# Layer 0 of a hybrid diffusion backbone: all tokens transposed first, more landing tiles, shift and scale wholly on TensorE

## The chip, the core and the metric

The kernel runs on one core of one Trainium2 chip. The engines are TensorE (PE; PEld is its weight load), VectorE (DVE), ScalarE (ACT), GpSimd (POOL) and SyncE (SP), which here issues the DMAs. The metric is the device time of one execution in microseconds, lower is better; times below are of the kernel before.

## What is computed

Four layers over 256 latent tokens and 256 context tokens of width 2048 in fp32. Layer i normalises (RMSNorm), applies shift and scale that come from a conditioning vector, mixes tokens (0: Fourier, 1: mLSTM, 2: attention, 3: Fourier), projects and adds with a gate. The start, which is all that the change touches, is this part:

```python
sc = jax.nn.silu(c)                                    # and sc_ctx = silu(c_ctx)
shift, scale, gate = jnp.split(sc @ ada_w[i] + ada_b[i], 3, axis=-1)
hx = _rmsnorm(x, norm_g[i]) * (1.0 + scale[:, None]) + shift[:, None]
...
def _fnet_branch(h, w_gate, w_out):
    return (_fourier_mix(h) * jax.nn.silu(h @ w_gate)) @ w_out
```

`ada_w[0]` is 2048 x 6144; its shift and scale columns are 33.5 MB, and no product with `w_gate` can start on a row of h before that row's shift and scale are known.

## The kernel before

Every large product is done by `gemm`: fp32 values are split into a high and a low part of a faster format (h and l of the activations, wh and wl of the weights), and three matmuls (h with wh, h with wl, l with wh) are added up. The reduction over 2048 runs in 16 tiles `kt`, taken as 8 pairs `k2`; one pair needs one weight tile of 512 KB, which `make_w` loads, splits on ScalarE (wh) and VectorE (wl), and hands out. A group of 512 output columns has four accumulator banks, so a pair is 24 matmuls of one group, called products here.

Layer 0 starts so: the conditioning vector is spread to all partitions (`spread`), the tokens `xt` are loaded in four tiles, their squares are summed on ScalarE (L585), and the reciprocal root r0 scales all of them on VectorE (L639). Then a loop over the 8 pairs (L640) makes shift and scale for the pair, in two pieces (SC and SH). A piece on TensorE, `ada_pe`, loads four landing tiles `araw` of 512 KB, multiplies them with the padded vector `cpad` (L187, 16 matmuls, each recorded as two by the profile), copies the result (`ar`), transposes it (L195) and adds up on VectorE. A piece on VectorE, `ada_dve`, loads four tiles of a transposed copy of the weights (`ada_t`) and makes two passes over each (L217). Both use the same four `araw` tiles. For pairs 2, 4 and 6 (`DV0`) the shift is made on VectorE, so 13 pieces are TensorE's and 3 are VectorE's.

What follows for a pair is the generator `turned(k2)`: for each of its two `kt` four transposes of the tokens (L615), the modulation from PSUM on ScalarE (`u`, L618), the split (L360, L361), and then the products of the pair before it. It is queued in the weave `fill`, which is advanced by one step for every 1/0.8 of a yield of the next pair's pieces. A second weave, `mixes`, advances the Fourier mixes of column blocks 0 to 2 (`mixed(j)`, eight yields each: four banks with L498, then two parities with L531, the first with L536) at 0.9 steps a yield. After pair 7 the rest of group 0 (`first`, with its last two pairs together, four times 12 products) and group 1 run, with what is left of the mixes woven in, and from there the gate's columns (`ga0`) on VectorE. `done_g` (L602) ends each column block of a group.

TensorE's program order is written by hand, as these generators yield; on the other engines a scheduler orders instructions. SP issues all DMAs in one order, and waits where a tile is still in use. Lines below are those of the kernel before; in the changed kernel the same statements stand some 10 to 40 lines lower (L187 is L197, L195 is L205, L298 is L308, L498 is L509, L531 is L542, the token transposes L615 are L637).

Of the kernel before, what the change touches and what calls it, by code (L numbers as in the profile page):

```python
# [14 lines left out]
P = 128  # L15
# [7 lines left out]
ARAW, WRAW, WHL = 4, 4, 3  # L23

DV0 = (2, 4, 6)

NPE1, CORE1, ATT = 4, 0.4, 1.2
MIX3, MIX0, MIX1, FR0, BR0, AR0 = 0.55, 0.9, 0.7, 0.8, 0.34, 0.17
# [23 lines left out]
def _build(tc, nc, top, A, out):  # L52
# [119 lines left out]

    def ada_pe(l, s, c, cpad, place):


        ps = bank()
        for k2 in range(2):
            raws = []
            for kq in (2 * k2, 2 * k2 + 1):
                pp, tag, bufs = next(place[0])  # L180
                raw = pp.tile([P, 2, 512], F32, tag=tag, name="araw", bufs=bufs)
                Q.dma_start(raw, A["ada_p"][l, s * 8 + c, kq])
                raws.append(raw.rearrange("p a b -> p (a b)").rearrange("p (q n) -> p q n", q=4))
            for i, rv in enumerate(raws):
                kq = 2 * k2 + i
                for q in range(4):
                    T.matmul(ps[32 * q:32 * q + 32, :256], cpad[:, 4 * kq + q, :], rv[:, q, :],  # L187
                             start=kq == 0, stop=kq == 3)
            yield 1
        r = ap_.tile([P, 256], F32, tag="ar", name="ar", bufs=1)  # L190
        S.copy(r, ps[:, :256])
        yield 1
        pt = bank()
        for i in range(2):
            T.transpose(pt[:, 128 * i:128 * i + 128], r[:, 128 * i:128 * i + 128], ident)  # L195
# [69 lines left out]
    def gemm(hl, orient, t0, t1, done, first=False, used=None, halves=False, begin=None):  # L265
# [46 lines left out]
        for k2 in range(2 if begin else 0, 6):  # L312
# [16 lines left out]
        wa, wb = next_w(), next_w()  # L329
        for kt in range(12, 16):  # L330
            hl[kt]
        yield "made"
        make_w()
        if halves:
            for s in range(2):
                for b in range(nb):
                    for kt in range(12, 16):
                        one(b, kt, wa if kt < 14 else wb, s)
# [5 lines left out]
        for b in range(nb):  # L344
            for kt in range(12, 16):
                one(b, kt, wa if kt < 14 else wb)
                if kt == 13:
                    yield
            done(b, banks[b][:, :n])
            yield  # L350
# [214 lines left out]
    with ExitStack() as st:  # L565
# [13 lines left out]
        for j in range(4):  # L579
# [3 lines left out]
            for i in range(4):  # L583
                junk = p0.tile([P, 512], F32, tag="mu2", name="junk", bufs=2)
                S.activation(junk, x[:, i, :], AF.Square, accum_out=ss[:, i, j:j + 1])  # L585
# [18 lines left out]

        with ExitStack() as st2:
            pf = pool(st2, "l0f", reuse_waits="tile")
            first = gemm(hl, "A", 0, 512, done_g, first=True)

            def turned(k2):

                for kt in (2 * k2, 2 * k2 + 1):
                    j, i = divmod(kt, 4)
                    ps = bank()
                    for t in range(4):
                        T.transpose(ps[:, 128 * t:128 * t + 128], xt[j][:, t, 128 * i:128 * i + 128], ident)  # L615
                    u = p0.tile([P, 512], F32, tag="mu2", name="u", bufs=2)
                    for s in range(2):
                        S.activation(u[:, 256 * s:256 * s + 256], ps[:, 256 * s:256 * s + 256], AF.Identity,  # L618
                                     scale=ada[:, 0, SC, s, kt:kt + 1], bias=ada[:, 0, SH, s, kt:kt + 1])
                    hl[kt] = split_into(kt, u)  # L620
                    yield
                if 0 < k2 <= 6:
                    for _ in range(4):
                        next(first)
                        yield
# [9 lines left out]
            mixes = Weave()  # L635
            slots = repeat((ap_, "araw", ARAW))
            for j in range(4):  # L637
                for i in range(4):
                    V.tensor_scalar(xt[j][:, i, :], xt[j][:, i, :], r0[:, i:i + 1], None, ALU.mult)  # L639
            for k2 in range(8):  # L640
                for s in (SC, SH):
                    for _ in ada_dve(0, s, 2 * k2, 2, 2) if s == SH and k2 in DV0 else ada_pe(0, s, k2, cpad, [slots]):
                        fill.give(FR0)
                        mixes.give(MIX0)
                fill.finish(f"t{k2 - 1}")
                fill.add(f"t{k2}", turned(k2))
                if k2 == 0:
                    Q.dma_start(cst[:, C_CD:], A["cst"][:, C_CD:])
# [6 lines left out]
            run(first, MIX1)  # L655
            order = [(s, j) for s in (SC, SH) for j in range(4)]
# [10 lines left out]
        place[0] = repeat((pa, "praw", 2))  # L667
# [703 lines left out]
```

## Time and profile before

| | |
|---|---|
| median of 3 runs | 2152.68 us (2150.70 to 2155.58) |
| the profiled execution | 2155.34 us, span 2153.5 us, mean granted clock 0.987 |
| first product of layer 0 (L298) | 54.61 us after the span's start |
| last piece of shift and scale on PE | 152.00 to 153.00 us |
| last `done_g` of group 0, of group 1 | 173.65 and 221.94 us |
| PE's waits for landing tiles, to 222 us | 12.7 us in 14 waits |

The span is the profiled time between the first and the last instruction; the rest of the execution's time lies around it. The rows of the page and of the trace on which the argument rests stand in the prediction.

### The profile page before, as it was taken

What the parts mean: (1) busy time and instruction counts of PE and PEld (TensorE: products, weight loads), DVE (VectorE), ACT (ScalarE), POOL (GpSimd) and SP (SyncE); (2) the same over time, 40 slices, a digit from 0 to 9 for tenths busy, and PEclk for the clock granted to TensorE, in tenths of its full rate; (3) what the DMA queues carried; (4) which work ended last, traced back from release to release, by engine and by line L of the source; (5) the groups of instructions that cost most, each with busy time, mean ns of one, the idle gap of its engine ahead of it and who ended that gap; (6) DMA issues with size and microseconds to landing.
All of it is one profiled execution on the core that took longest, in us unless ns stands there. A gap on an engine that the chain in (4) does not pass through costs nothing. (4 is left out here: it accounts for less than half of the span.)

```text
span 2153.5 us, 29391 instructions
## 1 busy us (share of the span) xinstructions
PE 2091.3 (97%) x11190; PEld 1725.9 (80%) x11190; DVE 1527.3 (71%) x2793; ACT 812.2 (38%) x1338; POOL 19.3 (1%) x29
## 2 busy tenths in 40 slices
PE   6899999999999999999999999999999999999998
PEld 2668777788788888888888888888787777999986
DVE  4867888856787787799666678765645665567666
ACT  4332242223333324232332343223336544545444
POOL 0000000000000000000000000000000000000000
PEclk7999999999999999999999999999999999999999
DMA  9775778872465565477668667983243454564464
GB/s 349 275 265 191 250 276 282 322 271 95 153 209 166 199 224 179 162 250 254 202 207 305 226 235 280 335 312 107 88 137 124 141 176 138 173 195 138 153 194 147
DMA packets 126127, 451.52 MB, mean 210 GB/s; under 512 B 14224, under 2 KB 16784, under 8 KB 123296
## 3 DMA queue, kind: packets, MB, share of 16 engines
q1 hardware_dynamic: 125696, 448.71, 61.0%
q8 instruction: 88, 1.44, 0.3%
q10 hardware_dynamic: 288, 0.92, 0.1%
q14 instruction: 55, 0.45, 0.1%
HBM read 435.91 MB, written 13.66 MB: 209 GB/s over the span
## 5 line engine op out<-in xcount | busy, mean ns | idle before, releaser
L257 DVE TENSOR_TENSOR wl<-wraw,wh 128x1024 fp32r<-128x1024 f32 x400 | 489.1, 1224 | 404.6 <-ACT wh L256 393.4
L298 PE MATMUL acc<-h,wh 128*128 128x512 f32 (+1 forms) x1936 | 689.3, 356 | 6.1 <-ACT h L395 3.9
L256 ACT CAST wh<-wraw 128x1024 fp32r<-128x1024 f32 x400 | 419.1, 1049 | 724.4 <-PE acc L298 581.4
L298 PE MATMUL acc<-l,wh 128*128 128x512 f32 (+1 forms) x1936 | 671.7, 347 | 3.0 <-DVE l L396 1.8
L298 PE MATMUL acc<-h,wl 128*128 128x512 f32 (+1 forms) x1936 | 670.4, 346 | 1.3 <-DVE wl L257 1.1
L298 PE MATMUL acc<-wh,h 128*128 128x512 f32 x1024 | 427.0, 417 | 3.5 <-DVE xn L1019 2.2
L298 PEld LDWEIGHTS acc<-h,wh 128*128 128x128 f32 x1936 | 367.8, 190 | 61.9 <-issue 11.2
L298 PEld LDWEIGHTS acc<-l,wh 128*128 128x128 f32 x1936 | 367.3, 190 | 51.2 <-DVE l L396 3.5
L298 PEld LDWEIGHTS acc<-h,wl 128*128 128x128 f32 x1936 | 367.9, 190 | 45.7 <-DVE wl L257 2.3
L298 PE MATMUL acc<-wh,l 128*128 128x512 f32 x1024 | 401.2, 392 | 0.5 <-DVE l L396 0.5
L298 PE MATMUL acc<-wl,h 128*128 128x512 f32 x1024 | 399.7, 390 | 0.0
L217 DVE SCALAR_TENSOR_TENSOR araw<-araw,cb 128x1024 f32<-128x1024 f32 x300 | 364.7, 1223 | 12.0 <-DMA araw<-in_ada_t_dram 9.8
L298 PEld LDWEIGHTS acc<-wh,h 128*128 128x128 f32 x1024 | 192.8, 188 | 52.0 <-issue 14.5
L298 PEld LDWEIGHTS acc<-wl,h 128*128 128x128 f32 x1024 | 193.0, 188 | 44.6 <-issue 8.4
L298 PEld LDWEIGHTS acc<-wh,l 128*128 128x128 f32 x1024 | 192.5, 188 | 42.8 <-DVE l L396 1.3
L217 DVE SCALAR_TENSOR_TENSOR ajunk<-araw,cb 128x1024 f32<-128x1024 f32 x172 | 209.8, 1220 | 0.0
L187 PE MATMUL xb<-araw,cpad 128*32 128x256 f32 x672 | 56.7, 439 | 15.4 <-DMA araw<-in_ada_p_dram 12.7
L187 PEld LDWEIGHTS xb<-araw,cpad 128*32 128x32 f32 x672 | 17.6, 116 | 44.9 <-DMA araw<-in_ada_p_dram 26.9
L395 ACT ACTIVATE h<-mu,ada 128x256 fp32r<-128x256 f32 x80 | 36.9, 502 | 35.9 <-DVE mu L394 35.9
L848 PE MATMUL xb<-v,wt 128*128 128x256 f32 x192 | 46.7, 379 | 0.0
L453 ACT ACTIVATE sq<-rn 128x256 f32<-128x256 f32 (+1 forms) x48 | 24.7, 515 | 56.1 <-DVE rn L447 54.3
L908 ACT ACTIVATE jk<-yp 128x256 f32<-128x256 f32 x32 | 13.3, 417 | 78.8 <-DVE yp L906 78.8
(223 smaller groups left out, 1480.3 us busy)
## 6 DMA issues: line engine op xcount, KB each, us to landing
araw<-in_ada_t_dram SPq DMA_DIRECT2D x300, 512.0 KB, 5.2
wraw<-in_w1in_dram SPq DMA_DIRECT2D x128, 512.0 KB, 4.4
araw<-in_ada_p_dram SPq DMA_DIRECT2D x84, 512.0 KB, 5.4
wraw<-in_w2in_dram SPq DMA_DIRECT2D x80, 512.0 KB, 3.5
wraw<-in_w0g_dram SPq DMA_DIRECT2D x32, 512.0 KB, 5.5
wraw<-in_w0o_dram SPq DMA_DIRECT2D x32, 512.0 KB, 5.7
wraw<-in_w1o_dram SPq DMA_DIRECT2D x32, 512.0 KB, 7.0
wraw<-in_w2o_dram SPq DMA_DIRECT2D x32, 512.0 KB, 4.2
```

Source lines behind the costliest of these rows:

```text
L187: T.matmul(ps[32 * q:32 * q + 32, :256], cpad[:, 4 * kq + q, :], rv[:, q, :], start=kq == 0, stop=kq == 3)
L217: V.scalar_tensor_tensor(o, rv, 1.0, cb[:, v + 2 - nv, part], ALU.mult, ALU.mult, accum_out=am[:, v, i, hf:hf + 1])
L256: S.copy(wh, raw)
L257: pace.append(V.tensor_tensor(wl, raw, wh.bitcast(F32), ALU.subtract).ins)
L298: T.matmul(o, lhsT, rhs, start=start, stop=stop)
L395: S.activation(h[:, c], u, AF.Identity, bias=ada[:, l, SH, s, kt:kt + 1])
L453: S.activation(sq[:, c], rn[:, b, c], AF.Square)
L848: T.matmul(po[:, :256], wt[:, 128 * k:128 * k + 128], c.v[:, k, 256 * hh:256 * hh + 256], start=k == 0, stop=k == nb - 1)
L908: S.activation(jk, ys, AF.Square, accum_out=c.ssq[:, 4 * hh + i:4 * hh + i + 1])
```

## The change

It concerns layer 0 up to the end of group 1.

- All shift and scale pieces of layer 0 are made by `ada_pe`; `DV0` is gone.
- `begin(0, ...)` weaves `turn(j)` into the two pieces of pair 0: it scales the tokens (half on ScalarE), transposes all 16 tiles and parks them as `xT` in the buffers of the later h tiles. `modulated(k2)` reads them from there.
- In `begin(k2)` the two pieces of pair k2 are woven with the products of pair k2-1 (six at a step, four steps), and otherwise with steps of the mixes. The weight tile is made at its beginning. `modulated(k2)` comes last.
- Landing tiles: pairs 0 to 2 cycle through six extra tiles (`l0l`) and the four `araw`; pairs 3 to 7 through the four `araw` and those buffers of l tiles 10 to 15 that are still free, each of which takes its 512 KB as two DMAs (`land_l`).
- The mixes of blocks 0, 1 and 2 are queued after pairs 3, 4 and 5 rather than 1, 3 and 5, at 1.0 step a yield, and what is left of them runs with group 0's last pair and group 1.
- Group 0 keeps one pair (`tail=1`) rather than two for its end.
- Half of the sums of squares go to VectorE, and the table for the root is loaded before the last token tile.

```diff
-DV0 = (2, 4, 6)
+ARAW, WRAW, WHL, LAND = 4, 4, 3, 6
-MIX3, MIX0, MIX1, FR0, BR0, AR0 = 0.55, 0.9, 0.7, 0.8, 0.34, 0.17
+MIX3, MIX0, MIX1, BR0, AR0 = 0.55, 1.0, 0.7, 0.34, 0.17
...
+    def land_l(kt):
+        def get(src):
+            raws = [hlp.tile([P, 512], F32, tag=f"l{k}", name=f"lraw{k}") for k in (kt, kt + 1)]
+            for i in range(2):
+                Q.dma_start(raws[i], src[:, i, :])
+            return raws
+        return get
...
-                junk = p0.tile([P, 512], F32, tag="mu2", name="junk", bufs=2)
-                S.activation(junk, x[:, i, :], AF.Square, accum_out=ss[:, i, j:j + 1])
+                if i % 2:
+                    junk = p0.tile([P, 512], F32, tag="mu2", name="junk", bufs=2)
+                    S.activation(junk, x[:, i, :], AF.Square, accum_out=ss[:, i, j:j + 1])
+                else:
+                    junk = ap_.tile([P, 1024], F32, tag="junk", name="ajunk", bufs=1)[:, :512]
+                    V.scalar_tensor_tensor(junk, x[:, i, :], 1.0, x[:, i, :], ALU.mult, ALU.mult,
+                                           accum_out=ss[:, i, j:j + 1])
+            if j == 2:
+                S.activation(dummy, ss[:, 1, 2:3], AF.Sqrt)
...
+        first = gemm(hl, "A", 0, 512, done_g, first=True, tail=1)
+        def turn(j):
+            for t in range(4):
+                if t % 2:
+                    S.activation(xt[j][:, t, :], xt[j][:, t, :], AF.Copy, scale=r0[:, t:t + 1])
+                else:
+                    V.tensor_scalar(xt[j][:, t, :], xt[j][:, t, :], r0[:, t:t + 1], None, ALU.mult)
+            for i in range(4):
+                ps = bank()
+                for t in range(4):
+                    T.transpose(ps[:, 128 * t:128 * t + 128], xt[j][:, t, 128 * i:128 * i + 128], ident)
+                x = hlp.tile([P, 512], F32, tag=f"h{4 * j + i}", name=f"xT{4 * j + i}")
+                (S.copy if i % 2 else V.tensor_copy)(x, ps)
+                xT.append(x)
+        def modulated(k2):
+            for kt in (2 * k2, 2 * k2 + 1):
+                u = p0.tile([P, 512], F32, tag="mu2", name="u", bufs=2)
+                for s in range(2):
+                    c = slice(256 * s, 256 * s + 256)
+                    S.activation(u[:, c], xT[kt][:, c], AF.Identity, scale=ada[:, 0, SC, s, kt:kt + 1],
+                                 bias=ada[:, 0, SH, s, kt:kt + 1])
+                hl[kt] = split_into(kt, u)
+        def begin(k2, places):
+            make_w()
+            place = [places]
+            for n, _ in enumerate(chain(*(ada_pe(0, s, k2, cpad, place) for s in (SC, SH)))):
+                if k2 == 0:
+                    if n % 2:
+                        turn(n // 2)
+                elif n in (1, 2, 5, 6):
+                    next(first)
+                else:
+                    mixes.give(MIX0)
+            modulated(k2)
+        with ExitStack() as st2:
+            pl = pool(st2, "l0l", reuse_waits="tile")
+            places = cycle([land(pl, "land", LAND)] * LAND + [araws] * ARAW)
+            for k2 in range(3):
+                begin(k2, places)
...
-            for k2 in range(8):
-                for s in (SC, SH):
-                    for _ in ada_dve(0, s, 2 * k2, 2, 2) if s == SH and k2 in DV0 else ada_pe(0, s, k2, cpad, [slots]):
-                        fill.give(FR0)
-                        mixes.give(MIX0)
-                fill.finish(f"t{k2 - 1}")
-                fill.add(f"t{k2}", turned(k2))
-                if k2 in (1, 3, 5):
-                    mixes.add("m", mixed(k2 // 2))
-            fill.finish("t7")
+            for k2 in range(3, 8):
+                spare = [land_l(kt) for kt in (10, 12, 14) if kt > 2 * k2]
+                begin(k2, cycle([araws] * ARAW + spare))
+                if k2 in (3, 4, 5):
+                    mixes.add("m", mixed(k2 - 3))
             while mixes.q:
                 fill.add("mix", mixes.q.pop(0)[1])
             fill.add("mix", mixed(3))
+            fill.step()
             run(first, MIX1)
```

First place: TensorE from pair 1's scale piece to the first products. Before, the pair's second piece is followed by token transposes of pair 1 (L615), banks of the first mix (L498) and then the products of `kt` 0:

```order
L187 MATMUL xb<-araw,cpad 32x256 x16
L615 MATMUL xb<-cst,xt 128x128 x4
L498 MATMUL xb<-cst,eo 128x128 x4
L615 MATMUL xb<-cst,xt 128x128 x4
L498 MATMUL xb<-cst,eo 128x128 x4
L195 MATMUL xb<-cst,ar 128x128 x2
L298 MATMUL acc<-h_338,wh 128x512
```

After the change, from the second piece of pair 0 on:

```order
L197 MATMUL xb<-araw,cpad 32x256 x16
L637 MATMUL xb<-cst,xt 128x128 x16
L205 MATMUL xb<-cst,ar 128x128 x2
L637 MATMUL xb<-cst,xt 128x128 x16
L197 MATMUL xb<-araw,cpad 32x256 x16
L308 MATMUL acc<-h_426,wh 128x512
L308 MATMUL acc<-h_426,wl 128x512
L308 MATMUL acc<-l_427,wh 128x512
```

The first products now stand behind three pieces instead of five, and all 64 token transposes stand before them; no mix has begun.

Second place: SP's queue from the last token tiles on. Before (the pieces of pairs 0, 1 and the first of 2, then the first VectorE piece):

```order
L581 DMA xt<-in_xtok_dram 128x2048 x3
L182 DMA araw<-in_ada_p_dram 128x1024 x8
L648 DMA cst<-in_cst_dram 128x1032
L182 DMA araw<-in_ada_p_dram 128x1024 x12
L253 DMA wraw<-in_w0g_dram 128x1024
L210 DMA araw<-in_ada_t_dram 128x1024 x4
L253 DMA wraw<-in_w0g_dram 128x1024 x3
```

After (`araw` stands for the extra landing tiles too, which bear the same name; `lraw` are the halves in l's buffers):

```order
L592 DMA xt<-in_xtok_dram 128x2048 x3
L263 DMA wraw<-in_w0g_dram 128x1024
L175 DMA araw<-in_ada_p_dram 128x1024 x8
L675 DMA cst<-in_cst_dram 128x1032
L263 DMA wraw<-in_w0g_dram 128x1024
L175 DMA araw<-in_ada_p_dram 128x1024 x8
L263 DMA wraw<-in_w0g_dram 128x1024
L175 DMA araw<-in_ada_p_dram 128x1024 x8
L263 DMA wraw<-in_w0g_dram 128x1024
L175 DMA araw<-in_ada_p_dram 128x1024 x4
L184 DMA lraw_721<-in_ada_p_dram 128x512
```

The weight tiles moved ahead of each pair's eight landing tiles, and no `ada_t` tile is left in this stage.

Third place: TensorE behind the last piece. Before, from the last product of pair 5:

```order
L298 MATMUL acc<-l_1094,wh 128x512
L615 MATMUL xb<-cst,xt 128x128 x8
L298 MATMUL acc<-h_1284,wh 128x512
L298 MATMUL acc<-h_1284,wl 128x512
L298 MATMUL acc<-l_1285,wh 128x512
L298 MATMUL acc<-h_1298,wh 128x512
```

After, from the last product of pair 6 (h_1414 is pair 7's first tile):

```order
L308 MATMUL acc<-l_1264,wh 128x512
L205 MATMUL xb<-cst,ar 128x128 x2
L542 MATMUL xb<-fU,cst 128x258 x2
L542 MATMUL xb<-fU,cst 128x126 x2
L542 MATMUL xb<-fU,cst 128x128 x2
L509 MATMUL xb<-cst,eo 128x128 x4
L308 MATMUL acc<-h_1414,wh 128x512
```

Before, pair 6's products and a mix bank stood between pair 7's transposes and its products; now one parity and one bank of mixes do.

More of the change, by code (lines that the diff above doesn't have):

```diff
@@ L177, in ada_pe @@
         for k2 in range(2):
[L178 to L183, printed above, removed]
+            raws = [next(place[0])(A["ada_p"][l, s * 8 + c, kq]) for kq in (2 * k2, 2 * k2 + 1)]
             for i, rv in enumerate(raws):
@@ L336, in gemm @@
                 for b in range(nb):
-                    for kt in range(12, 16):
-                        one(b, kt, wa if kt < 14 else wb, s)
+                    for kt in last:
+                        one(b, kt, ws[kt // 2 - 8], s)
                     if b % 2:
@@ L344, in gemm @@
         for b in range(nb):
-            for kt in range(12, 16):
-                one(b, kt, wa if kt < 14 else wb)
+            for kt in last:
+                one(b, kt, ws[kt // 2 - 8])
                 if kt == 13:
@@ L605, in _build @@
         with ExitStack() as st2:
             pf = pool(st2, "l0f", reuse_waits="tile")
[L607 to L625, printed above, removed]
```

35 lines of the change are left out of this document (19 added, 16 removed).

## The prediction

> **What bounds the kernel now.** I read the page first: busy shares, then the 40 slices.
>
> ```profile
> span 2153.5 us, 29391 instructions
> PE 2091.3 (97%) x11190; PEld 1725.9 (80%) x11190; DVE 1527.3 (71%) x2793; ACT 812.2 (38%) x1338; POOL 19.3 (1%) x29
> ...
> PE   6899999999999999999999999999999999999998
> ...
> PEclk7999999999999999999999999999999999999999
> ...
> GB/s 349 275 265 191 250 276 282 322 271 95 153 209 166 199 224 179 162 250 254 202 207 305 226 235 280 335 312 107 88 137 124 141 176 138 173 195 138 153 194 147
> ```
>
> The reader should see that PE is the bound everywhere but at the start, and that the first slice (54 us) has at once the lowest PE share, the lowest granted clock and the highest transfer rate, 349 GB/s. So I cut the start into stages; the columns are busy time of PE, PEld, DVE, ACT and POOL, then granted clock, DMA share and GB/s.
>
> ```profile
> 10.00:20.00 10.00, 5.61 (x40) 2.19 (x40) 5.22 (x15) 9.13 (x26) 0.00 (x0) 0.80 1.01 410
> 10.00:50.00 40.00, 27.16 (x199) 9.49 (x200) 16.62 (x46) 14.43 (x38) 0.00 (x0) 0.66 0.97 359
> 50.00:100.00 50.00, 43.58 (x309) 32.61 (x308) 39.29 (x93) 20.87 (x43) 0.00 (x0) 0.96 0.79 284
> 100.00:150.00 50.00, 41.23 (x300) 28.43 (x296) 34.50 (x98) 16.70 (x41) 0.00 (x0) 0.90 0.77 269
> 150.00:222.00 72.00, 70.82 (x358) 57.23 (x347) 51.99 (x105) 22.98 (x38) 0.00 (x0) 1.00 0.59 200
> 222.00:2153.50 1931.50, 1904.78 (x10028) 1594.72 (x10026) 1378.42 (x2443) 732.97 (x1170) 19.08 (x25) 1.00 0.60 203
> ```
>
> Between 10 and 150 us PE idles 12.8, 6.4 and 8.8 us, and until 50 us it runs at 0.66 of its clock. From 222 us on it idles 26.7 of 1931.5 us, 1.4%, at full clock. The change touches only work that ends by 222 us; what follows is PE-bound and woven by counts of yields, not by time, so whatever is won or lost at 222 us should arrive at the end unchanged. The transfers are the other resource: 97% busy until 50 us, then only 79% and 77%, though the next 33.5 MB of weights are known from the start. Who holds them back is in the waits of the DMA queue, and what PE waits for in its own (total us, times, longest):
>
> ```profile
> SPq L182 <- PE xb L187: 37.2, 29, 4.4
> SPq L182 <- DVE araw L217: 30.2, 9, 8.0
> ```
>
> ```profile
> PE xb L187 <- DMA araw<-in_ada_p_dram: 12.7, 14, 3.6
> PE xb L531 <- DVE fU L511: 2.5, 3, 1.1
> PE xb L531 <- ACT u L618: 1.8, 1, 1.8
> PE xb L531 <- ACT F L559: 1.8, 1, 1.8
> ```
>
> The queue waits for a landing tile to come free, 37 us for PE's pieces and 30 us for the VectorE pieces, while PE waits 12.7 us for landings. Four landing tiles are the throttle.
>
> **Prices, from the timeline.** (Start, duration, engine, line.)
>
> ```profile
> 54.61 0.51 PE L298 MATMUL acc<-h,wh 128*128 128x512 f32 x1 [2.26 <-ACT wh L256]
> ...
> 71.59 2.03 PE L531 MATMUL xb<-fU,cst 128*128 128x258 f32 x12 [1.84 <-ACT F L559]
> 73.54 1.07 PE L187 MATMUL xb<-araw,cpad 128*32 128x256 f32 x16
> ...
> 80.51 0.50 PE L298 MATMUL acc<-h,wh 128*128 128x512 f32 x1
> ...
> 83.39 0.38 PE L195 MATMUL xb<-cst,ar 128*128 128x128 f32 x2
> 83.70 1.07 PE L187 MATMUL xb<-araw,cpad 128*32 128x256 f32 x16
> 84.70 0.66 PE L615 MATMUL xb<-cst,xt 128*128 128x128 f32 x4
> ...
> 127.47 1.06 PE L498 MATMUL xb<-cst,eo 128*128 128x128 f32 x8
> 128.28 0.47 PE L298 MATMUL acc<-h,wh 128*128 128x512 f32 x1
> ```
>
> Matmuls overlap, so I price by starts. Half a piece of `ada_pe` (two landing tiles) takes 83.70 to 84.70, 1.0 us, and the two transposes 83.39 to 83.70, 0.3: **a piece costs PE 2.3 us**. From 80.51 to 83.39 run 12 products: 0.24 each, 5.8 us for a pair's 24. One Fourier bank takes 0.81, one parity of L531 71.59 to 73.54, 1.95: a mix is 4 x 0.81 + 2 x 1.95 + 0.3 for L536, 7.4 us.
>
> **Part 1, three pieces go from VectorE to TensorE.** PE gains 3 x 2.3 = 6.9 us. VectorE loses 3 x 8 passes over a tile, by this row 1.2 us each; they are hidden now except as holders of landing tiles (the 30.2 us above).
>
> ```profile
> L217 DVE SCALAR_TENSOR_TENSOR araw<-araw,cb 128x1024 f32<-128x1024 f32 x300 | 364.7, 1223 | 12.0 <-DMA araw<-in_ada_t_dram 9.8
> ```
>
> **Part 2, all tokens transposed in pair 0, landing in 10 tiles.** Pair 0 must scale 16 quarter tiles, half on each of two engines, copy 16 banks out, half each, and make the first h and l:
>
> ```profile
> L618 ACT ACTIVATE u<-xb,ada 128x256 f32<-128x256 f32 x32 | 16.4, 564 | 11.1 <-DVE ada L169 8.0 <-PE xb L615 3.0
> ...
> L361 DVE TENSOR_TENSOR l<-u,h 128x512 fp32r<-128x512 f32 x16 | 11.0, 690 | 18.9 <-ACT h L360 18.8
> ...
> L360 ACT CAST h<-u 128x512 fp32r<-128x512 f32 x16 | 9.9, 621 | 0.2
> L585 ACT ACTIVATE junk<-xt 128x512 f32<-128x512 f32 x16 | 9.9, 618 | 4.5 <-DMA xt<-in_xtok_dram 4.5
> ...
> L576 DVE COPY cb<-xb 128x512 f32<-128x512 f32 x8 | 5.1, 683 | 0.6 <-PE xb L236 0.6
> ```
>
> ```profile
> 19.52 6.43 DVE L639 TENSOR_SCALAR xt<-xt,r 128x512 f32<-128x512 f32 x16
> ```
>
> ScalarE is the longer side: from 19.5 us, 8 scalings and 8 copies at about 0.62 (the 128x512 row), 9.9, then u twice (1.1), h (0.6), l on VectorE (0.7) and some 1.5 for `ar` copies: the first product can run near 33 us, where now it waits until 54.6. The halved squares win little, since the last x tile still has to land first. Pair 1 costs PE 2 pieces and 24 products, 10.4 us at full clock, about 14 at the clock of this stretch: PE is through it at 47 us.
>
> **Part 3, the stream.** Up to the last piece's tiles SP must bring x (4.2 MB), constants (1.0), 9 weight tiles (4.7) and 64 landing tiles of 0.52 (33.5): 43.5 MB, 4.7 a pair. At the first slice's 349 GB/s, starting near 1.5 us, the last tile lands at 126 us; pair 3's last at 24.1 MB, 70.6 us. Six extra landing tiles in pairs 0 to 2, and in pairs 3 to 7 three, three, two, one and none beside the four, should keep it at that rate: SP then waits for tiles two pieces back, not one. Both ends for this rate: 410 GB/s (the 10 to 20 us row, partly in 8 KB rows of x) and 284 (50 to 100 us). I take 349, nearest to what the deeper queue is like, since the same `ada_p` tiles ran at 359 even with four slots when PE consumed at once. The half tiles of `land_l` (2 KB runs) have no row; I price them between the same and a tenth slower for 9 of 64 tiles, up to 1.5 us.
>
> The Trainium skill, page "DMA: Bandwidth & Descriptors", section "Bandwidth", measures 425 GB/s for large loads with one core running, and about 358 only as a core's share when its neighbour streams too. No row here holds 425; by it the 43.5 MB would be in by 104 us, and the stage would be PE's, which is the first rival below.
>
> **PE beside the stream.** Pairs 2 and 3 need 10.4 us of PE against 13.5 of transfers (4.7 MB): transfers lead, and PE ends pair 3 at 70.6 + 1.0 + 12 products (2.9) = 74.5. Pairs 4 to 7 add half a mix each: 14.1 us against 13.5, so PE leads by a little: 74.5 + 4 x 14.1 less the 12 products behind the last piece = 128.0. The waits in the mixes' chains (6.1 us for three mixes in the rows above) add some 2: **the last piece ends on PE at 130 us**. Now it ends at 153.0:
>
> ```profile
> 152.00 1.07 PE L187 MATMUL xb<-araw,cpad 128*32 128x256 f32 x16
> 153.00 0.50 PE L298 MATMUL acc<-h,wh 128*128 128x512 f32 x1
> ```
>
> That is 23 us earlier. **What is late next:** the remainder until column group 1 is done, whose last `done_g` now starts at
>
> ```profile
> 221.94 0.60 ACT L602 ACTIVATE sg<-acc 128x512 f32<-128x512 f32 x1 [0.30 <-PE acc L298]
> ```
>
> In program order this remainder now holds 252 products, 8 transposes, 4 Fourier banks and 2 parities; after the change 228 products, 8 banks and 5 parities: -5.8 - 0.8 (four take 0.66 above, the second four overlap) + 3.2 + 5.9 + 0.4 for one L536 = +2.9. Pair 7's h and l (2.4 us for u, h and l by the rows above, an estimated 1.2 for copy, transposes and reduce) are covered only by a parity and a bank (2.8 us), where now products of the pairs before cover them: about 0.6 stays open. Remainder +3.5. VectorE has two mixes beside the gate stream there, but 52 of 72 us busy now leaves 20 us of room for the one mix more; if it did not, L531's waits would grow, by 1 to 2 us each as above.
>
> **Sum:** -23 + 3.5 = -19.5 us. The profiled execution took 2155.34 us (span 2153.5), which makes 2135.8; the median of the three runs is 2.7 lower, so I predict **2133 us**.
>
> **Rivals.** (B) The stream runs at 410 GB/s or more; then PE leads from pair 1: 47 + 2 x 10.4 + 53.5 + 2 = 123 at the last piece, -30 + 3.5 = -26.5, 2126. For: the row at 410. Without any clock loss in pair 1 and without waits it is 118, 2121. (C) The tiles shrink again to four by pair 7, and PE frees them only after products and mix steps: the stream falls from 50 us on to the 284 GB/s of now. At 359 some 17.4 MB are in by then; the other 26.1 take 92 us, last piece 143, -10 + 3.5 = -6.5, 2146. For: 37.2 us of waits on PE. Against: the other 30.2 go with certainty, and the mixes leave pairs 2 and 3. (D) The clock: if PE's waits in pairs 2 and 3 keep it at 0.66, they cost 15.8 instead of 13.5 each, +4.6, 2138. Against: 0.96 already at 87% busy (50 to 100 us). The Trainium skill, page "TensorE: Matmul & The Clock Gate", part 1, lets the clock drop after an idle window of about 3.4 us; waits for two tiles are at most 3 us by the rate above, so by that rule D would not come. The waits of this trace, up to 3.6 us beside a clock of 0.66, do not settle it. (E) Slower: PE's program order, not the tiles, sets the pace. Every piece sits behind products or mix steps that wait on VectorE and ScalarE, so PE's lost time before 222 us stays what it is, only moved, and the 6.9 us of three more pieces come on top: 2160. It decides if PE's lost time falls by less than 6.9 of its 28 us idle (10 to 150 us) and the slow clock. Against: 12.7 us of that idle name landings. (F) It does not do what it says, tiles wait for others' pools and little moves: within 4 us.
>
> **How the numbers follow.** Forecast 0.50, B 0.17, C 0.12, D 0.08, E 0.07, F 0.06. The range goes from 2120 (the end of B) to 2148 (just past C); about 0.15 is left outside. 0.2% is about 4.3 us, what a measurement of this kernel can tell: faster (forecast, B, C, D) 0.87, same 0.06, slower 0.07.
>
> **What would show it.** First product near 33 us; DMA share over 0.9 until 120 us and 345 to 360 GB/s; SP's waits on VectorE's pieces gone from this stage; last piece at 130 us; last `done_g` of group 1 near 202; from there on the same distance to the end. Wrong would be: a DMA share under 0.8 before 120 us (C), PE gaps at L531's successors or at h of pair 7 above 5 us (E), or a start of products after 45 us.

## The result, and the profile after

The changed kernel takes 2129.78 us (median of 4 runs, 2128.92 to 2130.34) against 2154.13 us (4 runs, 2150.70 to 2156.11): 24.4 us less. The ratio of the runs is estimated at 0.9882 [0.987, 0.9894]; the two medians alone give 0.9887. Its profiled execution took 2128.92 us, span 2127.1.

The page after: span, the busy shares, and two rows of the 40 slices.

```profile
span 2127.1 us, 29564 instructions
PE 2083.3 (98%) x11292; PEld 1727.8 (81%) x11292; DVE 1508.7 (71%) x2761; ACT 817.8 (38%) x1342; POOL 20.4 (1%) x29
PE   7999999999999999999999999999999999999997
GB/s 395 333 242 210 293 256 302 323 191 96 179 188 163 221 244 169 162 272 248 186 240 262 236 239 299 334 288 107 89 148 111 151 176 131 184 194 136 150 198 148
```

The first two slices now move 395 and 333 GB/s (before: 349 and 275), and PE is at 90% or more from the second slice on (before: from the third). The windows of the start, with the same columns as before:

```profile
10.00:20.00 10.00, 5.91 (x32) 3.44 (x32) 8.99 (x24) 6.32 (x15) 0.00 (x0) 1.00 1.01 416
10.00:50.00 40.00, 32.98 (x272) 22.51 (x272) 25.38 (x60) 24.20 (x48) 0.00 (x0) 1.00 1.02 417
50.00:100.00 50.00, 49.05 (x412) 33.70 (x412) 24.54 (x66) 22.04 (x48) 0.00 (x0) 1.00 0.93 343
100.00:150.00 50.00, 47.00 (x332) 35.30 (x325) 35.52 (x89) 22.43 (x44) 0.00 (x0) 1.00 0.74 264
...
198.00:2127.10 1929.10, 1902.49 (x10031) 1593.35 (x10029) 1379.11 (x2443) 733.17 (x1171) 20.22 (x25) 1.00 0.60 203
```

PE idles 7.0, 1.0 and 3.0 us between 10 and 150 us, where it idled 12.8, 6.4 and 8.8. From 198 us on it does what it did from 222 us on: 1902.5 us of work and 26.6 us idle.

The clock in these rows needs care. The trace of this execution has no record of the granted clock before 30.9 us, and time without a record counts as full clock, so the 1.00 of the rows that start at 10 us is no measurement up to there. The pace of the matmuls in the timeline below has to be read instead. The waits of the DMA queue (first fence) and of PE (second) up to 135 and 200 us, in us, times and longest:

```profile
SPq L175 <- PE xb L197: 45.9, 19, 4.7
```

```profile
PE acc L308 <- ACT h L371: 2.7, 3, 1.2
PE xb L197 <- ACT wh L266: 2.6, 1, 2.6
PE xb L197 <- DMA araw<-in_ada_p_dram: 1.6, 3, 0.8
```

The queue no longer waits for a VectorE piece (30.2 us before). It still waits 45.9 us for PE to free tiles, but that now costs PE little: it waits 1.6 us for landings in all, where it waited 12.7. Some moments of the timeline:

```profile
17.83 3.44 PE L197 MATMUL xb<-araw,cpad 128*32 128x256 f32 x24 [2.56 <-ACT wh L266]
...
31.72 1.93 PE L197 MATMUL xb<-araw,cpad 128*32 128x256 f32 x32
...
39.31 0.50 PE L308 MATMUL acc<-h,wh 128*128 128x512 f32 x1
...
124.09 1.21 PE L197 MATMUL xb<-araw,cpad 128*32 128x256 f32 x13
132.35 0.50 PE L308 MATMUL acc<-h,wh 128*128 128x512 f32 x1 [1.21 <-ACT h L371]
...
198.62 0.60 ACT L621 ACTIVATE sg<-acc 128x512 f32<-128x512 f32 x1 [0.30 <-PE acc L308]
```

The first product runs at 39.3 us, the last piece ends at 125.3, and the last `done_g` of group 1 starts at 198.62 us, 23.3 us before its old place. I call this last time **the end of the stage** below, and use it beside the total time, since one profile shows it to a hundredth of a microsecond. It comes from one execution of each kernel, though, and the executions of one kernel lie 1.4 us (after) to 5.4 us (before) apart in total, so differences of one or two microseconds in it are not shown by themselves.

The stage can be read as a sum: its end is PE's busy time up to there plus PE's idle time. One window from 0 to the end of the stage gives both, here before and after:

```profile
0.00:221.94 221.94, 186.50 (x1163) 131.13 (x1164) 148.78 (x351) 79.22 (x169) 0.20 (x4) 0.91 0.75 268
```

```profile
0.00:198.62 198.62, 181.42 (x1265) 134.94 (x1266) 130.22 (x319) 84.91 (x173) 0.20 (x4) 1.00 0.81 299
```

Idle time fell from 35.4 to 17.2 us, and busy time fell too, from 186.5 to 181.4, although PE has 102 more matmul records (three pieces of 34) to do. The largest part of the idle time that is left, 7.7 us in three waits, lies before the first piece, where the conditioning vector is spread. The experiments ask which parts of the change bring these two sums.

The profiled pair differs by 26.4 us rather than 23.3. The other 3.1 us arise after the stage (1931.6 us remain before, 1928.5 after), in work that the change does not touch. There the execution before had dips of the granted clock that the one after did not have, for example 0.96 from 1960 to 2000 us, where the same 40 us of the program after (1935 to 1975 us) show 1.00.

### The profile page after: what moved, and what is told of

The parts are those of the page before. It is cut to its first block, busy times and chain, and to the rows that moved or that the text cites. A ratio compares the mean times of both kernels' runs of the same rounds, so it can differ in the third digit from the quotient of the medians.

```text
span 2127.1 us, 29564 instructions
## 1 busy us (share of the span) xinstructions
PE 2083.3 (98%) x11292; PEld 1727.8 (81%) x11292; DVE 1508.7 (71%) x2761; ACT 817.8 (38%) x1342; POOL 20.4 (1%) x29
## 5 line engine op out<-in xcount | busy, mean ns | idle before, releaser
L227 DVE SCALAR_TENSOR_TENSOR araw<-araw,cb 128x1024 f32<-128x1024 f32 x288 | 350.9, 1226 | 14.4 <-DMA araw<-in_ada_t_dram 12.1
L227 DVE SCALAR_TENSOR_TENSOR ajunk<-araw,cb 128x1024 f32<-128x1024 f32 x160 | 195.6, 1223 | 0.0
L197 PE MATMUL xb<-araw,cpad 128*32 128x256 f32 x696 | 48.5, 396 | 4.4 <-ACT wh L266 2.6
L891 PEld LDWEIGHTS xb<-v,wt 128*128 128x128 f32 x192 | 36.4, 189 | 6.1
```

Of the source, the lines that this page charges most:

```text
L227: V.scalar_tensor_tensor(o, rv, 1.0, cb[:, v + 2 - nv, part], ALU.mult, ALU.mult, accum_out=am[:, v, i, hf:hf + 1])
L891: T.matmul(po[:, :256], wt[:, 128 * k:128 * k + 128], c.v[:, k, 256 * hh:256 * hh + 256], start=k == 0, stop=k == nb - 1)
```

## The experiments

Eleven kernels ran, one of them twice. Ratios are to the kernel before, run on the same chip. None of them leaves out work.

### From the kernel before: the pieces, the tiles, both

**All pieces on TensorE**, nothing else:

```diff
-DV0 = (2, 4, 6)
+DV0 = ()
```

> The kernel before with all 16 pieces on TensorE and nothing else changed (four tiles, same order). If TensorE's time for three more pieces is what counts: plus 6.9 us, 2161. If VectorE's long holding of the landing tiles (30.2 us of SP's waits) was the worse cost: minus 3 to 8, 2146 to 2151. I lean to a wash, 2151 to 2158.

Measured: 2147.93 us, 0.9965 [0.9952, 0.9978]; stage end 215.21, 6.7 us earlier. That is not the wash to which I had leaned.

```profile
0.00:215.21 215.21, 189.78 (x1265) 131.51 (x1266) 122.89 (x303) 81.17 (x172) 0.20 (x4) 0.93 0.77 276
```

Busy rises by 3.3 us, idle falls by 10.0 to 25.4. The busy rise is mainly two things that work against each other, by the groups of pieces (L187) and parities (L531). Before, to 221.94 us:

```profile
L187 PE MATMUL xb<-araw,cpad 128*32 128x256 f32 x416 | 39.6, 472 | 15.4 <-DMA araw<-in_ada_p_dram 12.7 <-ACT junk L585 2.3
L531 PE MATMUL xb<-fU,cst 128*128 128x258 f32 (+2 forms) x96 | 19.4, 361 | 6.2 <-DVE fU L511 2.5 <-ACT u L618 1.8 <-ACT F L559 1.8
```

With all pieces on TensorE, to 215.21 us:

```profile
L187 PE MATMUL xb<-araw,cpad 128*32 128x256 f32 x512 | 46.0, 453 | 11.4 <-DMA araw<-in_ada_p_dram 11.2
L531 PE MATMUL xb<-fU,cst 128*128 128x258 f32 (+2 forms) x96 | 15.7, 312 | 0.0
```

The three pieces cost PE 6.4 us, as priced. But the parities' 6.2 us of waits for VectorE and ScalarE are gone, and their busy time is 3.7 us less. The waits for landings hardly change (12.7 to 11.2): SP no longer stands behind VectorE's pieces, but it now stands behind PE's tiles for 73.1 us instead of 37.2.

```profile
SPq L182 <- PE xb L187: 73.1, 44, 10.0
```

So in the old order VectorE's passes mainly held up the chains of the mixes, not the tiles. The waits that name ScalarE start at VectorE as well; before the parity at 106.10 us, ScalarE had itself waited for the shift and scale that VectorE finishes after its passes:

```profile
104.99 0.56 ACT L618 ACTIVATE u<-xb,ada 128x256 f32<-128x256 f32 x1 [5.26 <-DVE ada L169]
```

**More tiles**, with the VectorE pieces kept: each pair cycles through the four `araw` and the buffers of l tiles 10 to 15 that are still free, in pairs 0 to 2 those of h tiles 10 to 15 too.

```diff
+                if k2 in (0, 3, 4, 5, 6, 7):
+                    spare = [land_l(kt) for kt in (10, 12, 14) if kt > 2 * k2]
+                    if k2 < 3:
+                        spare += [land_l(kt, "h") for kt in (10, 12, 14)]
+                    ways = cycle([next(slots)] * ARAW + spare)
...
-                    for _ in ada_dve(0, s, 2 * k2, 2, 2) if s == SH and k2 in DV0 else ada_pe(0, s, k2, cpad, [slots]):
+                    for _ in ada_dve(0, s, 2 * k2, 2, 2) if s == SH and k2 in DV0 else ada_pe(0, s, k2, cpad, [ways]):
```

> The kernel before, its order and its three VectorE pieces kept, with extra landing tiles for the TensorE pieces: six (three pairs of l buffers, three of h buffers) in pairs 0 to 2, then the same l buffers as in the change. Theory T: PE's 12.7 us of waits for landings and the slow clock of 10 to 50 us go, minus 12 to 18 us, 2136 to 2142. Rival R: PE's order holds it, within 4 us of before, 2150 to 2157.

Measured: 2151.24 us, 0.9975 [0.9966, 0.9985]; stage end 220.01, 1.9 us earlier.

```profile
10.00:50.00 40.00, 28.63 (x219) 12.08 (x217) 19.32 (x53) 18.71 (x46) 0.00 (x0) 0.83 1.03 400
50.00:100.00 50.00, 43.17 (x302) 31.22 (x302) 39.46 (x95) 16.61 (x34) 0.00 (x0) 0.97 0.82 282
```

```profile
SPq L177 <- DVE araw L229: 32.9, 9, 8.5
```

The tiles lift the rate until 50 us from 359 to 400 GB/s. From 50 us on it is 282, as before (284): SP still stands 32.9 us behind tiles that VectorE holds (30.2 before). Tiles alone are worth little.

**Both** (`DV0 = ()` on top of the tiles):

> The kernel before with the extra landing tiles and all pieces on TensorE, its order kept (transposes pair by pair, products two pairs behind, mixes from pair 1 on). Theory T: most of the change's gain, 2132 to 2140. Rival R: 2150 or more. If it ends between 2140 and 2148, supply and order each carry a half.

Measured: 2141.67 us, 0.9934 [0.9917, 0.995]; stage end 212.23, 9.7 us earlier.

```profile
0.00:212.23 212.23, 190.37 (x1265) 133.62 (x1266) 122.39 (x303) 80.48 (x171) 0.21 (x4) 0.94 0.78 280
```

So pieces and tiles bring 9.7 of the 23.3 us in the old order; the remaining 13.6 come with the rest of the change, the new order above all. Of the 13.6, by the two window rows, 9.0 are busy time (190.37 to 181.42) and 4.7 idle (21.9 to 17.2).

### From the changed kernel: take one part out

**Four landing tiles only:**

```diff
-            places = cycle([land(pl, "land", LAND)] * LAND + [araws] * ARAW)
+            places = cycle([araws] * ARAW)
...
-                spare = [land_l(kt) for kt in (10, 12, 14) if kt > 2 * k2]
+                spare = []
```

> The changed kernel with only the four landing tiles of before (no extra tiles in pairs 0 to 2, none of the l buffers after). Theory T (the supply was the throttle, the tiles lifted it): the stream falls from the 417 and 343 GB/s of the changed kernel (10 to 50, 50 to 100 us) towards 360 and 285, PE waits for landings more than 10 us again, the last piece ends near 143 us instead of 125, and the time is 2145 to 2150, most of the gain lost. Rival R (the order on TensorE carried it: transposes first, one pair's products earlier, mixes later): four tiles do as well with this order, 2130 to 2134, PE's waits for landings under 5 us.

Measured: 2142.74 us, 0.9943 [0.9928, 0.9957]; stage end 212.10, 13.5 us later than after.

```profile
0.00:212.10 212.10, 187.43 (x1265) 135.01 (x1266) 130.20 (x319) 85.37 (x172) 0.21 (x4) 0.94 0.78 280
10.00:50.00 40.00, 31.27 (x240) 20.56 (x240) 26.02 (x59) 22.25 (x44) 0.00 (x0) 0.83 0.89 334
50.00:100.00 50.00, 43.06 (x344) 26.50 (x343) 17.92 (x45) 19.74 (x39) 0.00 (x0) 0.90 0.89 318
```

The rate falls to 334 and 318 GB/s, and idle time rises by 7.5 us, as one expects. Busy time rises too, by 6.0, for the same 1265 matmuls. One place in its timeline shows how, with the window of the slow row behind it:

```profile
64.78 0.64 PE L197 MATMUL xb<-araw,cpad 128*32 128x256 f32 x8
66.50 0.64 PE L197 MATMUL xb<-araw,cpad 128*32 128x256 f32 x8 [1.08 <-DMA araw<-in_ada_p_dram]
68.75 1.08 PE L197 MATMUL xb<-araw,cpad 128*32 128x256 f32 x8 [1.62 <-DMA araw<-in_ada_p_dram]
70.01 1.08 PE L197 MATMUL xb<-araw,cpad 128*32 128x256 f32 x8 [0.17 <-DMA araw<-in_ada_p_dram]
```

```profile
68.75:70.00 1.25, 1.08 (x8) 0.20 (x8) 0.51 (x1) 0.00 (x0) 0.00 (x0) 0.50 0.80 249
```

Eight records take 0.64 us; after two waits of 1.1 and 1.6 us the same eight take 1.08, at a granted clock of 0.50. **A wait can be paid twice**: as idle time, and in the pace of what follows it. The total, 2142.74 us, lies just below the range of theory T (2145 to 2150) and far above its rival's.

**The shift of pairs 2, 4 and 6 back on VectorE**, run twice; the profile shown is of the second run:

```diff
-            for n, _ in enumerate(chain(*(ada_pe(0, s, k2, cpad, place) for s in (SC, SH)))):
+            for n, _ in enumerate(chain(*(ada_dve(0, s, 2 * k2, 2, 2) if s == SH and k2 in (2, 4, 6)
+                                          else ada_pe(0, s, k2, cpad, place) for s in (SC, SH)))):
```

> The changed kernel with the shift pieces of pairs 2, 4 and 6 on VectorE again (in the four araw tiles), all else as changed. Theory P (from the first product on TensorE leads, the stream has slack): 6.9 us less of TensorE's time come off the end, 2123 to 2126, last piece near 119 us. Rival S (VectorE holds its landing tiles for two passes and SP's one queue stops behind them, as in the kernel before): slower, 2131 to 2140, PE waits for landings of the next pieces more than 5 us. From the kernel before, where taking these pieces away won 8 us though TensorE got more work, I lean to S, 2134.

> A second look at dve_pieces_back, whose profiled execution ran at a clock of 0.60: time near 2158 again. If SP's one queue is what costs, SP waits over 25 us in all for tiles that VectorE or a piece in front holds, the transfers fall below 300 GB/s between 50 and 125 us, and TensorE's waits for landings come to more than 10 us. If TensorE is instead held by VectorE's results (am, ada, l), its waits name those and the transfers stay above 330 GB/s.

Measured: 2158.64 us, 1.0017 [1.0008, 1.0027]; the second run took 2155.61, stage end 222.92, 24.3 us later than after. The whole gain is gone, and the time lies 19 us above the slowest that I had expected (2140). The windows of the second run, then the waits of its queue and of PE:

```profile
0.00:222.92 222.92, 185.05 (x1163) 134.84 (x1164) 157.22 (x367) 83.95 (x169) 0.20 (x4) 0.89 0.73 266
50.00:100.00 50.00, 36.17 (x240) 22.36 (x240) 33.39 (x70) 14.86 (x29) 0.00 (x0) 0.82 0.89 313
```

```profile
SPq L220 <- PE xb L197: 20.0, 8, 6.4
SPq L175 <- DVE araw L227: 18.6, 8, 7.0
```

```profile
PE xb L197 <- DMA araw<-in_ada_p_dram: 16.4, 12, 4.8
PE acc L308 <- ACT h L371: 5.2, 4, 2.5
PE xb L197 <- DVE fU L519: 3.3, 1, 3.3
```

SP issues in one order. The loads of a VectorE piece (L220) must wait until PE has freed a tile, 20.0 us; the loads of the next PE piece (L175) then stand behind tiles that VectorE holds for two passes, 18.6 us. PE has nothing else to do meanwhile: it waits 16.4 us for landings, and from 50 to 100 us it is busy 36.2 of 50 us at a clock of 0.82. Idle time is 20.7 us more than in the changed kernel (37.9 against 17.2). Of this, 14.8 us are landings; the other 5.8 are waits for h (2.7 us in the changed kernel) and for VectorE's fU (none there), so late results of ScalarE and VectorE have a part too. Busy time rises by 3.6 us although 102 records are gone, which is pace again. One of the three signs that I had named for the queue did not come: the transfers ran at 312 GB/s from 50 to 125 us, not below 300. In this order the three pieces are the dearest single item that was tried.

**Tokens not parked**: each pair transposes its own two tiles, and ScalarE modulates from PSUM, as before.

```diff
-                x = hlp.tile([P, 512], F32, tag=f"h{4 * j + i}", name=f"xT{4 * j + i}")
-                (S.copy if i % 2 else V.tensor_copy)(x, ps)
-                xT.append(x)
...
-                    S.activation(u[:, c], xT[kt][:, c], AF.Identity, scale=ada[:, 0, SC, s, kt:kt + 1],
+                    S.activation(u[:, c], ps[:, c], AF.Identity, scale=ada[:, 0, SC, s, kt:kt + 1],
```

> The changed kernel with all tokens scaled in pair 0 but transposed pair by pair at the end of each pair's pieces, modulated from PSUM; no parked copies. Theory I (parking does 6.3 us of transposes in TensorE's idle, slow-clocked start): all but the first pairs' transposes come on top of a stretch that TensorE leads, plus 3 to 6, 2133 to 2136, first product near 35 us instead of 39.3. Rival: the first product comes earlier by as much as the transposes cost later, 2128 to 2131.

Measured: 2130.94 us, 0.9883 [0.9868, 0.9898]; first product at 36.0 us, stage end 201.19.

**Products two pairs behind**, as before the change:

```diff
-        first = gemm(hl, "A", 0, 512, done_g, first=True, tail=1)
+        first = gemm(hl, "A", 0, 512, done_g, first=True)
...
-                elif n in (1, 2, 5, 6):
+                elif k2 > 1 and n in (1, 2, 5, 6):
```

> The changed kernel with the products two pairs behind the pieces, as before the change, and group 0 ending with two pairs (tail=2). Theory O (early products are what the new order wins: TensorE idles until they start): first product near 44 to 50 us, plus 5 to 9, 2135 to 2139. Rival: TensorE does the same pieces sooner instead and the stream at 417 GB/s keeps up, within 2 us, 2128 to 2132.

Measured: 2131.01 us, 0.9885 [0.987, 0.99]; first product at 46.9 us, stage end 199.37.

**Half the tokens parked in pair 0, the rest in pair 1:**

```diff
-                    if n % 2:
-                        turn(n // 2)
+                    if n in (1, 5):
+                        turn(n // 4)
...
+                elif k2 == 1:
+                    if n in (3, 7):
+                        turn(2 + n // 4)
```

> The changed kernel with pair 0's shift piece ahead of the second token block's transposes, and blocks 2 and 3 transposed in pair 1 instead of pair 0. Theory: the first product comes near 35 us instead of 39.3 and TensorE's full work starts sooner, minus 1 to 4, 2126 to 2129. Rival: the same work is only permuted, 2129 to 2131; if the chain to the first h is bound by ScalarE's scalings, the first product stays at 38 or later.

Measured: 2128.79 us, 0.9875 [0.986, 0.989]; first product at 36.2 us, stage end 199.95. The interval covers the changed kernel's ratio, so it is no better version.

Of these three, no total can be told from the changed kernel's, so theories I and O, by which the undone edits cost 3 to 9 us, fall. The first product moved between 36.0 and 46.9 us, and the end of the stage by 0.8 to 2.6 us. So the place of the first product, on which the prediction put so much, hardly sets the time by itself.

**Both undone** (not parked and two behind), to see whether the two stand in for each other:

> The changed kernel with both undone at once: transposes pair by pair (not parked) and products two pairs behind; tiles, pieces, weight tile first and late mixes as changed. Theory F (TensorE has idle, slow-clocked time to about 45 us, and any ready work fills it: parked transposes or early products, each replaces the other, so undoing one costs nothing and undoing both does): first product at 47 us or later, 6 to 11 us slower than the changed kernel, 2136 to 2141, near the kernel before with tiles and all pieces on TensorE (2141.7). Rival M (what separates that kernel from the changed one is the late start of the mixes or the weight tile's early load): within 2 us of the changed kernel, 2128 to 2133.

Measured: 2134.33 us, 0.9893 [0.9877, 0.9909]; first product at 48.1 us, stage end 204.72, 6.1 us later than after, where the two alone cost 2.6 and 0.8.

```profile
0.00:204.72 204.72, 181.86 (x1265) 133.04 (x1266) 125.53 (x311) 79.98 (x164) 0.20 (x4) 0.99 0.78 290
```

They do in part: 5.7 of the 6.1 us are idle time (22.9 against 17.2). The total, 2134.33 us, lies between the two ranges that were expected (2128 to 2133 and 2136 to 2141), and its ratio alone cannot be told from the changed kernel's; the reading rests on the stage. Early transposes of all tokens and early products are two ways to give PE something to do between the first landings. With one of them there is nearly enough.

**Pair 0's weights ahead of the tokens**: SP brings the eight landing tiles of pair 0 into l buffers before the tokens, and the two pieces run first.

```diff
+        early = [iter([land_l(kt) for kt in range(0, 16, 2)])]
+        for s in (SC, SH):
+            drain(ada_pe(0, s, 0, cpad, early))
...
+            if k2 == 0:
+                for j in range(4):
+                    turn(j)
+                modulated(0)
+                return
```

> The changed kernel with pair 0's eight landing tiles loaded into the sixteen l buffers ahead of the token tiles, its two pieces first on TensorE, and all four turns behind them. TensorE idles until 17.8 us in the changed kernel, waiting for what lies behind x; two pieces (4.6 us, more at the slow clock) go there. Theory F: minus 2 to 5, 2125 to 2128. Rival: x lands some 10 us later, r0 and with it every turn, and the first product moves to 42 us or more, 2130 to 2136.

Measured: 2139.73 us, 0.9917 [0.9899, 0.9935]; first product at 45.8 us, stage end 205.97. That is slower than both ranges that were expected. The pieces at the start had to wait, and the transposes, which start at 34.8 us instead of 23.5, had nothing ahead of them to fill PE's time. This leaves two holes (waits of PE, to 222 us; the profile names no releaser for the longer one):

```profile
PE xb L638 <- issue: 7.9, 1, 7.9
PE xb L197 <- DMA lraw<-in_ada_p_dram: 7.2, 1, 7.2
```

### From the old order towards the new: the mixes later

The new order with both halves undone still ends the stage 7.5 us earlier than the old order with tiles and all pieces on TensorE (204.72 against 212.23). A candidate was the place of the mixes, which the old order begins after pair 1.

```diff
-MIX3, MIX0, MIX1, FR0, BR0, AR0 = 0.55, 0.9, 0.7, 0.8, 0.34, 0.17
+MIX3, MIX0, MIX1, FR0, BR0, AR0 = 0.55, 0.5, 0.7, 0.8, 0.34, 0.17
...
-                if k2 in (1, 3, 5):
-                    mixes.add("m", mixed(k2 // 2))
+                if k2 in (3, 4, 5):
+                    mixes.add("m", mixed(k2 - 3))
```

> The kernel before_tiles_all_pe with the mixes as late and as thin as in the changed kernel: queued after pairs 3, 4 and 5, half a step a yield. It still transposes pair by pair, has its products two pairs behind and loads its weight tiles late. Theory M (mixes that start after pair 1 hold TensorE's order, and with it the landing tiles, while pieces are the scarce work): group 1 ends near 205 us after the span's start as in both_undone, not at 212, and the time is 2133 to 2137. Rival W (the rest: weight tile first, split squares and scalings, whole instead of half landing tiles): no change, 212 us and 2140 to 2143.

Measured: 2145.33 us, 0.9948 [0.993, 0.9966]; stage end 213.41, 1.2 us later than without it.

```profile
0.00:213.41 213.41, 190.32 (x1265) 131.60 (x1266) 122.33 (x303) 80.44 (x172) 0.20 (x4) 0.96 0.76 279
```

The last row of the pieces in its timeline:

```profile
131.12 1.16 PE L199 MATMUL xb<-araw,cpad 128*32 128x256 f32 x16
```

The candidate falls (the time is even above both ranges that were expected), and the run teaches something else: the last piece ends at 132.3 us, 11 us earlier than without the edit (143.3), and the stage ends no earlier. Work that leaves the time before the last piece stands behind it. The last piece is a milestone, not the bound; PE's busy plus idle time is.

Where the 7.5 us sit can still be read. Busy time falls by 8.5 us (190.37 to 181.86) and idle rises by 1.0. Most of it is in the piece matmuls. Here are the windows of these alone (their busy time and number, granted clock, DMA): old order with tiles and all pieces on TensorE, new order with both undone, changed kernel. The clock record of the second begins at 30.8 us, that of the third at 30.9.

```profile
0.00:212.23 212.23, 45.55 (x512) 0.94 0.78 280
```

```profile
0.00:204.72 204.72, 39.01 (x512) 0.99 0.78 290
```

```profile
0.00:198.62 198.62, 35.76 (x512) 1.00 0.81 299
```

The same 512 records take 45.6, 39.0 and 35.8 us. In the first of the three kernels a large part stands in one stretch at full clock:

```profile
29.83:45.05 15.22, 11.24 (x92) 1.00 1.05 398
```

```profile
41.05 4.00 PE L199 MATMUL xb<-hraw,cpad 128*32 128x256 f32 x24
```

At 1.93 us for 32 records, the row of the changed kernel above, 92 records would take 5.5 us. The 24 records at 41.05 us use six half tiles of 256 KB in 4.00 us, 0.67 us each; at the 398 GB/s of this stretch one half lands in 0.66 us. So here PE goes at the pace of the landings, in waits too short to show as idle time, and busy time holds them. Which of the edits that are left brings the difference (the weight tile issued ahead of its pair, products written between the pieces rather than advanced by `fill`, whole extra tiles instead of halves in pairs 0 to 2, the split squares and scalings) was not tried apart and stays open.

## Why the prediction was right, and where it was not

The sign, the range and the size were right: 2133 us forecast, 2129.8 measured. Its main claims held: the landing tiles and VectorE's pieces throttle the start, PE's wait for landings goes, and what is won at the end of the stage (23.3 us) arrives at the end (24.4 us by the medians). But the case that came is nearer to rival B (the faster stream, PE in the lead) than to the forecast, and several terms missed, partly in opposite directions: the first product came 6 us late, while the stream and PE's work beside it were faster than priced. That the total came within 3.2 us is in part luck.

| term | predicted | measured |
|---|---|---|
| first product | 33 us | 39.3 us |
| rate of the stream, 10 to 50 us | 349 GB/s | 417 GB/s |
| last piece ends on PE | 130 us, -23 | 125.3 us, -27.8 (from 153.1) |
| from there to the end of the stage | 72.4 us, +3.5 | 73.3 us, +4.4 |
| end of the stage | about 202 us, -19.5 | 198.6 us, -23.3 |

**Part 1, the VectorE pieces, was the step that failed.** Its price for PE was right: 6.9 us predicted, 6.4 measured in the old order. But I called VectorE's passes "hidden now except as holders of landing tiles" and gave their removal no term of its own. In the old order their removal alone wins 6.7 us: the waits in the chains of the mixes (6.2 us), the parities' own time (3.7) and some 4 us of the pieces' own waits go, against 6.4 us of added work. Those waits stood in my rows, and I even kept "some 2" of them for the new order, where none is left. In the new order the same removal is worth 24.3 us, most of it through the queue.

**Part 2, the first product,** was late by 6 us because I followed ScalarE's chain. On the timeline PE sets it: 64 transposes and three pieces stand ahead, and until 31 us they run at half pace or less (24 records of a piece in 3.44 us at 17.8 us, 32 in 1.93 us at 31.7). The step also mattered less than I thought: the three runs that each undo or vary one edit spread the first product over 11 us and the stage by at most 2.6.

**Part 3, the stream,** was mis-sized: ten tiles in flight ran at 417 GB/s, not 349, and only fell to 343 from 50 us on, when PE led. My row of 359 GB/s with four tiles was itself limited by the tiles: more tiles in the old order lifted it to 400, and four tiles in the new order ran at 334. The Trainium skill, page "DMA: Bandwidth & Descriptors", section "Bandwidth", gives 425 GB/s for a 16 MB load with one core alone; the 417 GB/s of this trace agree within 2%, and by that sentence I should have weighted rival B higher. The half tiles' price cannot be seen in the changed kernel: PE hardly waited for landings.

**PE beside the stream.** With the stream in front, PE leads from the first product on: it is busy 49.1 of 50 us from 50 to 100. I had transfers lead in pairs 2 and 3 and two microseconds of waits in the mixes; neither came. Rival B put the last piece at 123 us; it came at 125.3, and what makes the 2 us was not traced.

**The remainder** was right to 0.9 us, the wait for pair 7's h (1.21 us, I had 0.6) included. **The way to the end** was right: the difference at the stage's end stays.

**The other rivals.** C (tiles shrink, the stream falls) did not come: 343 and 264 GB/s after 50 us, but with PE in the lead. D (the clock stays low) did not come in the changed kernel, where no dip is on record from 30.9 us to the end of the stage. In the run with four tiles it came in part: 0.90 from 50 to 100 us, and a halved pace at 68.75 us after waits of at most 1.62 us. The rule that I cited from the Trainium skill, page "TensorE: Matmul & The Clock Gate", part 1, speaks of an idle window of about 3.4 us; these rows show the pace fall after shorter single waits that come close together, so the rule did not exclude D. E (PE's program order sets the pace) did not decide: between 10 and 150 us PE's idle time fell from 28.0 to 11.0 us, far more than 6.9. F is refuted by the total.

What the sum had only for pair 1 is the pace. Elsewhere I priced a piece by its full-speed row and multiplied. PE's piece matmuls took 39.6 us for 416 records before and 35.8 us for 512 after, so that the added work was more than paid by the faster pace of all of it.

## What to carry to other kernels

Where one in-order queue feeds two engines through shared buffers, ask what the queue stands behind: the engine that frees a buffer late stops the loads of the other one too, and moving its work away can be worth far more than its own time (6.7 us in one order, 24.3 in another, for 6.4 us of added work). Parts of such a change hold each other up: tiles without the pieces won 1.9 us, and the changed kernel without the extra tiles lost 13.5, so trying them one by one can throw out a good change. Count a stage as busy plus idle time of its bounding engine, and look at both, since a wait can also slow the matmuls that follow it, and busy time can hold waits too short to show as idle; milestones such as the first product or the last piece can move by 11 us with hardly anything behind them.

## What the runs showed of the hardware that was not expected

- One core's loads, from 10 to 50 us mostly in 512 KB tiles, ran at 417 GB/s (DMA share 1.02) with ten landing tiles to fill; with four the same stretch showed 334.
- TensorE's pace halved after waits of 1.08 and 1.62 us (eight piece records in 0.64 us, then in 1.08 at a granted clock of 0.50).
- The clock of the profile's rows can lack a record at the start: in the changed kernel the row from 10 to 20 us reads 1.00, while 24 piece records took 3.44 us at 17.83 us, against 1.93 us for 32 at 31.72 us. Its trace has no record of the clock before 30.9 us.
